# Moving a matmul's streamed operand by 192 bytes: x and its forms from 224 to 32 modulo 256 in a two-layer hybrid decoder

## The chip, the cores and the metric

The kernel runs on one core of one Trainium2 chip. The metric is the device time of one execution in microseconds (us); shown is the median of three runs. The engines are TensorE (PE; its weight loads are a row of their own, PEld), VectorE (DVE), ScalarE (ACT), GpSimd (POOL) and SyncE (SP), which issues the loads from device memory.

## What is computed

Two decoder layers over 512 tokens of width 1024, in float32. Each layer is a half-step SwiGLU FFN, a token mixer (sparse attention, NSA, in layer 0; the gated recurrence HGRN2 in layer 1) and a second half-step FFN, each followed by a layer norm:

```python
def _swiglu(x, w_gate, w_up, w_down):
    return (jax.nn.silu(x @ w_gate) * (x @ w_up)) @ w_down

for i in range(DEPTH):
    x = _layer_norm(alpha * x + 0.5 * _swiglu(x, ffn1 of layer i), ...)
    y = _nsa(x, ...) if kind == 0 else _hgrn2(x, ...)
    x = _layer_norm(alpha * x + y, ...)
    x = _layer_norm(alpha * x + 0.5 * _swiglu(x, ffn2 of layer i), ...)
```

The FFN's inner width is 2816. The mixers project x by `w_in` (NSA: queries, keys, values, gates; HGRN2: four times 1024 columns) and their output by `w_out`.

## The kernel before, in words

Every float32 operand of a large product is held as two parts, `hi` and `lo` (ACT rounds a copy, DVE subtracts), and `mm3` (lines 126 to 130) makes a product of three matmuls: hi by hi, lo by hi or hi by lo, and so on. A row such as `ps<-xh,whi` names the moving operand first (streamed column by column) and then the stationary one (loaded ahead as weights). A matmul has 128 rows of contraction and 256 or 512 columns.

x is kept transposed in `xh` and `xl` (made by `new_xt`, line 79), in a pool `xt` at the upper end of SBUF. Weights come through SP into `raw`, and are split into the ring `whi`/`wlo` or, in the FFN, into two further buffers `xhi`/`xlo`; the last weights of a `down` or of an output projection go into a pool `wl`.

The FFN (`ffn_body`, line 248) takes 22 blocks of 128 inner columns in two halves, 12 and then 10. Blocks go in pairs. The first pair of the first half is `plain_pair`. All others are `seven`: seven products of half-size blocks instead of eight, on x's four quarters (moving `xh`/`xl`) and on three sums of quarters, the forms `t0h` to `t2l` (variable `tf`, in a pool `mid`). A product is 2 x 4 calls of `mm3` on 256 columns. The weights' sums are formed in `fr`, also in `mid`, as are `sg`, `p1`, `q2`, `q3` and `c`. So the first half has one plain pair and five of `seven`, the second half five of `seven`; after each half, `down` multiplies the 12 or 10 blocks of `h` (stationary parts `xhi`/`xlo`) by `w_down` (moving, 512 columns), 8 PSUM banks at once.

Elsewhere x is moving in `proj_t` (512 columns in two pieces; NSA's compression, keys and queries, HGRN's queries) and stationary in `tok_proj` (HGRN's other three projections, weights moving, 512 columns), in NSA's value projections (256 and 304 columns) and in NSA's output projection, for which `o_t` writes the attention's output into `xh`/`xl`. HGRN's output projection has its own stationary tiles, `oth`/`otl`.

PE's program stands in the order in which it is written; the other engines' order is set by a scheduler.

`gap` (line 74) takes a tile that nobody uses, so that what stands behind it in its pool starts later.

Of the kernel before, what the change touches and what calls it, by code (L numbers as in the profile page):

```python
# [55 lines left out]
class Trunk:  # L56
# [22 lines left out]
    def new_xt(self):  # L79

        self.free_xt()
        self.xt = ExitStack()
        pool = self.xt.enter_context(self.tc.tile_pool(name="xt", bufs=1, side="right", reuse_waits="tile"))
        self.xh = pool.tile([P, 2, NK, 2 * P], F32R, name="xh")
        self.xl = pool.tile([P, 2, NK, 2 * P], F32R, name="xl")

    def xr(self, k, c0=0, c1=NT):

        s = slice(c0 // 2, c1 // 2)
        return self.xh[:, s, k, :], self.xl[:, s, k, :]  # L90
# [158 lines left out]
    def ffn_body(self, pool, wg, wu, wd, gb_idx, out):  # L249
        nc = self.nc  # L250
        self.gap(pool, 128)
        h = pool.tile([P, 12, T], F32, name="h")

        self.wx = pool, 2
        w3 = [w.rearrange("(k p) f -> p k f", p=P) for w in (wg, wu)]
        LASTU = 4
        with ExitStack() as es:
            mid = es.enter_context(self.tc.tile_pool(name="mid", bufs=1, reuse_waits="tile"))
            self.gap(mid, 192)
            tf = [[mid.tile([P, 4, 256], F32R, name=f"t{n}{x}") for x in "hl"] for n in range(3)]  # L260

            hq = h.rearrange("p j t -> p (j t)")
            xb = hq[:, 2048:4096].rearrange("p (a k t) -> p a k t", a=2, k=4)
            f1, f2 = (hq[:, 1024 * n : 1024 * n + 1024].rearrange("p (k t) -> p k t", k=4) for n in (4, 5))
            for half, (f0, nf) in enumerate(((0, 12), (12, 10))):
                for pr in range(nf // 2):
                    g = f0 // 2 + pr
                    if g < NSTD:
                        if g == 0:
                            for k in range(2):  # L270
                                ks = slice(4 * k, 4 * k + 4)
                                nc.gpsimd.tensor_tensor(xb[:, k], self.xh[:, 0, ks].bitcast(F32), self.xl[:, 0, ks].bitcast(F32), op=ALU.add)
                            self.forms = xb, f1, f2
                        self.plain_pair(mid, w3, g, h[:, 2 * pr : 2 * pr + 2, :])
                        if g == 0:
                            self.forms = None
                            for (hi, lo), src in zip(tf, (f1, f2, xb[:, 0])):
                                self.split(hi, lo, src)
                        if g == NSTD - 1:
                            self.split(self.xh[:, 1, 0:4], self.xl[:, 1, 0:4], xb[:, 1])  # L280
                    else:
                        self.seven(mid, tf, w3, g, h[:, 2 * pr : 2 * pr + 2, :], g >= NSTD + 2)
                if half == 0:
                    banks = self.down(wd, h, f0, nf, nf, None)
                    for c in range(NT):
                        for x in range(2):
                            s = slice(512 * x, 512 * x + 512)
                            nc.vector.scalar_tensor_tensor(self.x[c][:, s], self.x[c][:, s], 2.0 * ALPHA, banks[c][x], op0=ALU.mult, op1=ALU.add)
        with ExitStack() as es:
            wl = es.enter_context(self.tc.tile_pool(name="wl", bufs=4, reuse_waits="tile"))  # L290
            gb = self.ln_params(*gb_idx, [wl.tile([P, D], F32, name=n, bufs=1) for n in ("lng", "lnb")])
            banks, last = self.down(wd, h, f0, nf, nf - LASTU, wl)
            self.finish(last, banks, gb, 4.0 * LN_EPS, out)
# [971 lines left out]
```

## Time and profile before

| | |
|---|---|
| median of 3 runs | 2103.89 us (2103.47 to 2104.97) |
| the profiled execution | 2099.54 us, its span 2097.8 us |
| PE busy | 2055.2 us, 98% |
| PEld busy | 1885.4 us, 90% |
| DVE busy | 1418.3 us, 68% |
| ACT busy | 976.1 us, 47% |
| granted clock of TensorE, mean | 0.995 |

Busy is the time in which an engine has at least one instruction in hand. Matmuls overlap: the record of one lasts longer than the distance to the next. The idle time in a row of the groups is that of the engine ahead of these instructions, with what ended it.

The first FFN's halves of `seven` lie at about 30 to 133 and 199 to 297 us, the second FFN's at 725 to 833 and 897 to 996, the third's at 1070 to 1176 and 1242 to 1341, the fourth's at 1765 to 1868 and 1934 to 2034; a `down` follows each. NSA runs from 353 to 705 and HGRN from 1396 to 1745.

### The profile page before, as it was taken

Reading aid. Unit: us, or ns where it says so; the run is one execution under the profiler, and the core shown is the slowest. Engines: PE = TensorE matmul, PEld = TensorE weight load, DVE = VectorE, ACT = ScalarE, POOL = GpSimd, SP = SyncE. Lnnn points to the kernel's source line nnn. Section 1 sums busy time; section 2 is a strip of 40 time slices with the busy share of each in tenths; the row PEclk is TensorE's granted clock in tenths of the full one; section 3 lists DMA queues with packets and bytes.
Section 4 is the critical chain, followed back from the end, with each engine's and each line's share of the span. In section 5 each row is a group of like instructions: output and inputs, shape, how many; then the busy total and the mean of one; then the engine's idle time right before and its main releaser. Section 6 shows DMA issues by size and latency. Waiting matters only on the chain.

```text
span 2097.8 us, 34590 instructions
## 1 busy us (share of the span) xinstructions
PE 2055.2 (98%) x14277; PEld 1885.4 (90%) x14277; DVE 1418.3 (68%) x2124; ACT 976.1 (47%) x1570; POOL 217.2 (10%) x321
## 2 busy tenths in 40 slices
PE   8999999999999999999999999999999999999998
PEld 8998998879898899899899989988788989998996
DVE  8946855377775896486598467664636858955864
ACT  5543552255565354255345335435536734543551
POOL 1000002001122300000110000021321213000002
PEclk9999999999999999999999999999999999999999
DMA  5441342231011145133234412512231023342331
GB/s 181 122 150 51 102 145 76 82 110 41 31 31 51 61 125 157 48 113 115 67 121 124 138 57 86 172 60 90 82 116 31 2 71 101 115 147 61 101 121 41
DMA packets 138762, 194.00 MB, mean 92 GB/s; under 512 B 8571, under 2 KB 117435, under 8 KB 138604
## 3 DMA queue, kind: packets, MB, share of 16 engines
q1 hardware_dynamic: 138604, 191.79, 29.6%
q8 instruction: 112, 1.84, 0.4%
q14 instruction: 46, 0.38, 0.1%
HBM read 189.58 MB, written 2.19 MB: 91 GB/s over the span
## 4 chain that ended last, share of the span: by engine, by line
PE 83%; DVE 10%; POOL 2%; ACT 2%; issue 1%; DMA 1%; DVEq 0%; POOLq 0%; SPq 0%; ACTq 0%
PE ps L128 23%; PE ps L130 23%; PE ps L129 23%; PE po L820 3%; DVE wlo L113 2%; PE ps L804 2%; PE ps L1148 1%; DVE raw L350 1%; PE sc L771 1%; PE sc L772 1%; DVE st L201 1%; DVE x L200 1%; PE ps L543 1%; DVE xl L113 1%; ACT whi L112 1%
## 5 line engine op out<-in xcount | busy, mean ns | idle before, releaser
L113 DVE TENSOR_TENSOR wlo<-raw,whi 128x1024 fp32r<-128x1024 f32 (+1 forms) x253 | 315.2, 1250 | 275.0 <-ACT whi L112 274.3
L112 ACT ACTIVATE whi<-raw 128x1024 fp32r<-128x1024 f32 (+1 forms) x253 | 265.6, 1055 | 359.7 <-PE ps L130 164.5
L128 PE MATMUL ps<-xh,whi 128*128 128x256 f32 (+1 forms) x1120 | 332.9, 297 | 3.0 <-ACT whi L112 1.6
L130 PE MATMUL ps<-xh,wlo 128*128 128x256 f32 (+1 forms) x1120 | 331.1, 296 | 2.3 <-DVE wlo L113 2.3
L129 PE MATMUL ps<-xl,whi 128*128 128x256 f32 (+1 forms) x1120 | 331.0, 296 | 1.2 <-DVE xl L113 1.2
L130 PE MATMUL ps<-whi,xlo 128*128 128x512 f32 x704 | 274.4, 390 | 1.5 <-DVE xlo L113 1.5
L128 PE MATMUL ps<-whi,xhi 128*128 128x512 f32 x704 | 274.4, 390 | 0.0
L129 PE MATMUL ps<-wlo,xhi 128*128 128x512 f32 x704 | 274.0, 389 | 0.0
L130 PEld LDWEIGHTS ps<-xh,wlo 128*128 128x128 f32 x1120 | 212.3, 190 | 10.2 <-DVE wlo L113 2.8
L128 PEld LDWEIGHTS ps<-xh,whi 128*128 128x128 f32 x1120 | 210.8, 188 | 11.8 <-ACT whi L112 2.0
L129 PEld LDWEIGHTS ps<-xl,whi 128*128 128x128 f32 x1120 | 211.0, 188 | 8.9 <-DVE xl L113 1.8
L128 PE MATMUL ps<-xh,xhi 128*128 128x256 f32 x640 | 180.2, 282 | 7.3 <-DVE q L404 7.2
L112 ACT ACTIVATE whi<-fr 128x1024 fp32r<-128x1024 f32 x120 | 126.7, 1059 | 118.6 <-PE ps L129 83.8
L129 PE MATMUL ps<-xl,xhi 128*128 128x256 f32 x640 | 179.8, 281 | 0.0
L130 PE MATMUL ps<-xh,xlo 128*128 128x256 f32 x640 | 179.8, 281 | 0.0
L113 DVE TENSOR_TENSOR wlo<-fr,whi 128x1024 fp32r<-128x1024 f32 x120 | 146.8, 1224 | 47.4 <-ACT whi L112 47.1
L130 PEld LDWEIGHTS ps<-whi,xlo 128*128 128x128 f32 x704 | 132.2, 188 | 30.7 <-DVE xlo L113 3.2
L129 PEld LDWEIGHTS ps<-wlo,xhi 128*128 128x128 f32 x704 | 132.2, 188 | 26.8
L128 PEld LDWEIGHTS ps<-whi,xhi 128*128 128x128 f32 x704 | 132.2, 188 | 26.8
L350 DVE TENSOR_TENSOR raw<-fr 128x1024 f32<-128x1024 f32 x120 | 145.8, 1220 | 13.1 <-DMA fr<-in_ffn_w_up_dram 11.4
L113 DVE TENSOR_TENSOR xlo<-h,xhi 128x1024 fp32r<-128x1024 f32 x44 | 53.9, 1226 | 111.8 <-ACT xhi L112 111.8
L128 PEld LDWEIGHTS ps<-xh,xhi 128*128 128x128 f32 x640 | 121.6, 190 | 8.1 <-DVE q L404 7.8
(267 smaller groups left out, 4737.7 us busy)
## 6 DMA issues: line engine op xcount, KB each, us to landing
raw<-in_ffn_w_down_dram SPq DMA_DIRECT2D x88, 512.0 KB, 3.5
fr<-in_ffn_w_gate_dram SPq DMA_DIRECT2D x80, 512.0 KB, 4.0
fr<-in_ffn_w_up_dram SPq DMA_DIRECT2D x80, 512.0 KB, 5.0
raw<-in_hgrn_w_in_dram SPq DMA_DIRECT2D x32, 512.0 KB, 4.2
raw<-in_nsa_w_in_dram SPq DMA_DIRECT2D x18, 512.0 KB, 3.9
raw<-in_ffn_w_gate_dram SPq DMA_DIRECT2D x8, 512.0 KB, 5.4
raw<-in_ffn_w_up_dram SPq DMA_DIRECT2D x8, 512.0 KB, 4.5
raw<-in_nsa_w_out_dram SPq DMA_DIRECT2D x8, 512.0 KB, 3.4
```

Source lines behind the costliest of these rows:

```text
L112: a = self.nc.scalar.activation(hi, src, AF.Copy)
L113: b = self.nc.vector.tensor_tensor(lo, src, hi.bitcast(F32), op=ALU.subtract)
L128: mm(out, l[0], r[0], start=start, stop=False)
L129: mm(out, l[0], r[1], start=False, stop=False)
L130: mm(out, l[1], r[0], start=False, stop=stop)
L200: nc.vector.scalar_tensor_tensor(x[:, s], x[:, s], float(scale), banks[h], op0=ALU.mult, op1=ALU.add)
L201: nc.vector.bn_stats(st[:, h, :], x[:, s])
L350: tt(out, x, y, op=op)
L543: nc.tensor.matmul(ph, w1[:, j, :], self.ap(z[:, 0:1], 2 * j, [[16, 129]]), start=j == 0, stop=j == 15)
L771: nc.tensor.matmul(sc[:, t - ts[0], :], l, kh[t][g][:, :n], start=True, stop=False)
L804: nc.tensor.transpose(p[:, j * P : j * P + P], pf[:, (b0 + j) * P : (b0 + j + 1) * P], self.ident)
L820: nc.tensor.matmul(po[:, ii, t, :], pt[:, t * (i + 1) + j, :], v[j][:, t, g, :], start=j == 0, stop=j == i)
```

## The change

One gap leaves pool `mid`, and one of the same size enters pool `xt`:

```diff
@@ new_xt
         self.xh = pool.tile([P, 2, NK, 2 * P], F32R, name="xh")
         self.xl = pool.tile([P, 2, NK, 2 * P], F32R, name="xl")
+        self.gap(pool, 192)
@@ ffn_body
             mid = es.enter_context(self.tc.tile_pool(name="mid", bufs=1, reuse_waits="tile"))
-            self.gap(mid, 192)
             tf = [[mid.tile([P, 4, 256], F32R, name=f"t{n}{x}") for x in "hl"] for n in range(3)]
```

Pool `xt` ends at the upper end of SBUF, so the new gap moves `xh` and `xl` down by 192 bytes (196576 to 196384 and 212960 to 212768); what stands in `mid` moves down by 192 as well. No other tile moves. The starts of the tiles modulo 256 bytes in the two programs (the steps within these tiles are multiples of 256):

| tiles | before | after |
|---|---|---|
| `xh`, `xl` | 224 | 32 |
| `t0h` to `t2l`, `fr`, `sg`, `p1`, `q2`, `q3`, `c` (pool `mid`) | 224 | 32 |
| `raw`, the ring `whi`/`wlo`, the FFN's `xhi`/`xlo`, `h`, its `wl`, x itself | 32 | 32 |
| `wl` of NSA's output projection | 0 | 0 |
| `wl` of HGRN's output projection, `oth`/`otl` | 160 | 160 |

The instructions and their order are the same on every engine. Two waits differ, both in the last FFN, since tiles of `mid` now lie over other tiles of the stage before: ACT's split into `t1h` loses a wait for a load, and on SP's queue the third pair of loads of `fr` gains one for PE. SP's rows there, before:

```order
L343 DMA fr<-in_ffn_w_gate_dram 128x4x256 [waits PE_49]
L343 DMA fr<-in_ffn_w_up_dram 128x4x256 [waits DMAHW6_49]
L343 DMA fr<-in_ffn_w_gate_dram 128x4x256 [waits DMAHW7_49]
L343 DMA fr<-in_ffn_w_up_dram 128x4x256
L343 DMA fr<-in_ffn_w_gate_dram 128x4x256
L343 DMA fr<-in_ffn_w_up_dram 128x4x256 [waits DMAHW2_49]
```

and after (names ending in `_49` are the program's semaphores: PE's, and those of single load queues):

```order
L343 DMA fr<-in_ffn_w_gate_dram 128x4x256 [waits PE_49]
L343 DMA fr<-in_ffn_w_up_dram 128x4x256 [waits DMAHW6_49]
L343 DMA fr<-in_ffn_w_gate_dram 128x4x256 [waits DMAHW7_49]
L343 DMA fr<-in_ffn_w_up_dram 128x4x256
L343 DMA fr<-in_ffn_w_gate_dram 128x4x256 [waits PE_49]
L343 DMA fr<-in_ffn_w_up_dram 128x4x256 [waits DMAHW2_49]
```

Nothing moved; the fifth load waits for PE, for the last but one matmul of HGRN's output projection, for which the first of these loads already waited in the program before.

## Rows read from the trace of the kernel before

**Rows 1.** The page, busy time of PE, its share and instructions.

```profile
PE 2055.2 (98%) x14277; PEld 1885.4 (90%) x14277; DVE 1418.3 (68%) x2124; ACT 976.1 (47%) x1570; POOL 217.2 (10%) x321
```

**Rows 2.** The page, the chain that ended last, by engine.

```profile
PE 83%; DVE 10%; POOL 2%; ACT 2%; issue 1%; DMA 1%; DVEq 0%; POOLq 0%; SPq 0%; ACTq 0%
```

**Rows 3.** Windows of `seven`: length, busy (count) of PE, PEld, DVE, ACT, POOL, clock, DMA.

```profile
200.00:296.00 96.00, 96.00 (x817) 96.00 (x817) 71.98 (x74) 51.39 (x69) 0.00 (x0) 1.00 0.33 99
...
900.00:990.00 90.00, 90.00 (x766) 90.00 (x766) 66.94 (x69) 48.08 (x66) 0.00 (x0) 1.00 0.32 95
...
1100.00:1170.00 70.00, 70.00 (x620) 70.00 (x619) 55.20 (x60) 38.17 (x51) 0.00 (x0) 1.00 0.48 148
1245.00:1340.00 95.00, 95.00 (x809) 95.00 (x809) 70.71 (x73) 51.18 (x68) 0.00 (x0) 1.00 0.32 97
...
1936.00:2030.00 94.00, 94.00 (x801) 94.00 (x800) 70.60 (x74) 50.61 (x68) 0.00 (x0) 1.00 0.32 96
```

**Rows 4.** First of PE's groups, 1100 to 1170 us: count, busy, mean ns, idle before.

```profile
L128 PE MATMUL ps<-xh,whi 128*128 128x256 f32 x64 | 17.7, 276 | 0.0
```

**Rows 5.** The same group of PE, 200 to 296 us.

```profile
L128 PE MATMUL ps<-xh,whi 128*128 128x256 f32 x78 | 21.9, 281 | 0.0
```

**Rows 6.** Timeline of PE at the seam of `down` and `seven`: start, duration.

```profile
198.89 0.39 PE L130 MATMUL ps<-whi,xlo 128*128 128x512 f32 x1
199.12 0.28 PE L128 MATMUL ps<-xh,whi 128*128 128x256 f32 x1
199.24 0.28 PE L129 MATMUL ps<-xl,whi 128*128 128x256 f32 x1
199.35 0.28 PE L130 MATMUL ps<-xh,wlo 128*128 128x256 f32 x1
```

**Rows 7.** Windows, PE alone: `down`, `tok_proj`, HGRN's `proj_t` (PE, clock, DMA).

```profile
1557.50:1587.50 30.00, 30.00 (x130) 1.00 0.28 88
...
1415.00:1497.00 82.00, 82.00 (x360) 1.00 0.30 93
136.00:196.00 60.00, 60.00 (x267) 1.00 0.17 52
```

**Rows 8.** Timeline of PE, HGRN's output projection, ring weights: first and last of 14.

```profile
1708.14 0.39 PE L128 MATMUL ps<-whi,oth 128*128 128x512 f32 x1
...
1711.17 0.40 PE L129 MATMUL ps<-wlo,oth 128*128 128x512 f32 x1
```

**Rows 9.** The same, weights from `wl`: first and last of 9.

```profile
1724.15 0.39 PE L129 MATMUL ps<-wlo,oth 128*128 128x512 f32 x1
...
1725.96 0.39 PE L128 MATMUL ps<-whi,oth 128*128 128x512 f32 x1
```

**Rows 10.** Groups of PE by form, whole span; one of the three lines of `mm3`.

```profile
L128 PE MATMUL ps<-whi,xh 128*128 128x512 f32 x256 | 100.7, 393 | 0.0
...
L128 PE MATMUL ps<-xh,whi 128*128 128x512 f32 x160 | 64.1, 400 | 0.3 <-DVE qs L713 0.3
```

**Rows 11.** Groups of PE, 748.1 to 750.3 us, behind a stall.

```profile
L128 PE MATMUL ps<-xh,xhi 128*128 128x256 f32 x7 | 2.1, 296 | 2.5 <-DVE q L404 2.5
L129 PE MATMUL ps<-xl,xhi 128*128 128x256 f32 x7 | 2.0, 281 | 0.0
```

**Rows 12.** Groups of PE, 752 to 755 us.

```profile
L129 PE MATMUL ps<-xl,xhi 128*128 128x256 f32 x6 | 1.7, 276 | 0.0
```

**Rows 13.** The page, DVE's subtraction by its source.

```profile
L113 DVE TENSOR_TENSOR wlo<-raw,whi 128x1024 fp32r<-128x1024 f32 (+1 forms) x253 | 315.2, 1250 | 275.0 <-ACT whi L112 274.3
...
L113 DVE TENSOR_TENSOR wlo<-fr,whi 128x1024 fp32r<-128x1024 f32 x120 | 146.8, 1224 | 47.4 <-ACT whi L112 47.1
```

**Rows 14.** Timelines of PE and SP at the fourth FFN's start.

```profile
1744.99 0.39 PE L129 MATMUL ps<-wlo,oth 128*128 128x512 f32 x1
...
1747.47 0.77 SPq L343 DMA_DIRECT2D fr<-in_ffn_w_gate_dram  x1
```

## The prediction

> **What bounds the kernel now.** I read the page first: PE is busy 98% of the 2097.8 us span [rows 1] and has 83% of the chain that ended last [rows 2]. Busy is no measure of pace, since a matmul's record includes its way through the array, so I asked at which distance matmuls start. In a stretch where PE has no idle time, the pace is (length of the window + length of one record) / count, because a record that reaches over the window's edge is counted too.
>
> The main loop of each FFN is `seven`, with 256 columns per matmul, run five times before the first `down` and five times after it: same code, same shapes, same buffers. Before `down`, in the row of 1100 to 1170 us: (70.00 + 0.276) / 620 = 113.35 ns [rows 3, 4]. After it: (96.00 + 0.281) / 817 = 117.85 ns, and by the same sum 117.86, 117.78 and 117.70 ns in the other three FFNs [rows 3, 5]. Nobody is waited for in either: idle before each group is 0.0 [rows 4, 5], the granted clock is 1.00, PE is busy for the whole window [rows 3]. So the slow halves do not wait for an instruction; each matmul itself takes 4.4 ns more. The seam shows when it begins: `down` ends at 0.23 us a matmul of 512 columns, and from the very next one, without a gap, starts are 0.11 to 0.12 us apart [rows 6], the pace of the whole half.
>
> What the slow stretches share is the offset, modulo 256 bytes, of their two operands, which PE streams (moving) and loads (stationary) at the same time: PEld is as busy as PE in rows 3. The table of offsets stands in the section on the change. In pace per 512 columns:
> - `down`, 32 against 32: (60.00 + 0.389) / 267 = 226.2 ns [rows 7]
> - `tok_proj`, moving 32, stationary 224: (82.00 + 0.391) / 360 = 228.9 ns [rows 7]
> - `proj_t`, moving 224, stationary 32: (30.00 + 0.394) / 130 = 233.8 ns [rows 7]
> - the HGRN output projection, stationary 160: with the weights of the ring, at 32, 13 intervals take 3.03 us, 233 ns [rows 8]; with the weights of `wl`, at 160, 8 intervals take 1.81 us, 226 ns [rows 9].
>
> The last pair is the best experiment in this trace: same line, shape and stationary tiles, and only the moving operand's offset differs. Equal offsets run at 226 ns, unequal ones at 229 to 234.
>
> **The change part by part.** It moves `xh`/`xl` and all of pool `mid` from 224 to 32, so that every pair of `seven`, `proj_t` and `tok_proj` becomes 32 against 32. No instruction is added, removed or reordered.
>
> (a) Second halves of the FFNs: 5 pairs x 7 products x 8 x 3 = 840 matmuls, four times, 3360. If they run at the first halves' pace, each gives 117.8 - 113.4 = 4.4 ns: 14.8 us. All of it lies on the path, as PE never idles there. Cover: DVE, the next busiest, has 71.98 of 96 us; at the first halves' pace it has 55.20 of 70, 79%, and PE still has no idle time there [rows 3], so the inputs arrive in time. The bounds are 0 (the pace stays) and 14.8; I take 14.8, since equal offsets in rows 7 and 9 are the nearest rows.
>
> (b) `tok_proj`: 3 x 192 = 576 of the 768 matmuls of 512 columns whose stationary is x [rows 10] (256 on each of three lines; the other 192 are NSA's output projection), each 228.9 - 226.2 = 2.7 at most and 228.9 - 226.7 = 2.2 by two intervals of the 113.35 pace: 1.3 us.
>
> (c) `proj_t` on 512 columns: 160 x 3 = 480 matmuls [rows 10]. 144 are HGRN's queries, on the path: 7 ns each, 1.0 us. 48 stand in NSA's compression: 0.3 us. 288 stand among the attention's units, where PE also waits for others; between 0 and 2.0 us, I take 1.0.
>
> (d) NSA's value projections, 96 of 256 and 96 of 304 columns with x stationary: no clean stretch; between 0 and the 4.4 ns of the second halves, 0.8 us, which I take. Output projection, 192: the half whose weights come from the ring becomes 32 against 32, 96 x 5 ns = 0.5 us; the other half has `wl` at 0 against 224 now and against 32 then, a pair that no row shows: between -0.6 and +0.6 us, 0 taken.
>
> (e) First halves are at 113.35 already: 0.
>
> (f) `fr`, the `sg` tiles and `c` move too, and DVE and ACT read or write them. The same subtraction takes 1250 ns from `raw` (at 32) and 1224 ns from `fr` (at 224) [rows 13]; DVE has slack, and I put it at nothing.
>
> (g) On SP's queue the third pair of loads of the last FFN gains a wait for PE. It waits for the last but one matmul of the HGRN output projection; the first pair, ahead of it in the queue, waited for that already. It was issued at 1747.47 us, 2.48 us after that matmul started [rows 14]. Behind it stand the other loads of that FFN. Price 0.
>
> Sum: 14.8 + 1.3 + 2.3 + 1.3 = 19.7 us. The profiled execution took 2099.54 us (span 2097.8 and 1.7 around it); the median of the three timed runs is 2103.89, 4.4 more, and I take the gain from the median: 2084.2.
>
> **The rivals.**
>
> *The pace depends on how a stretch is entered, not on the offsets.* For it: the first halves have the same unequal offsets and run at 113 ns. The middle of FFN 2's first half shows the jump: after a stall of 2.5 us the records are 281 ns long, the slow kind, and three microseconds later, after another short stall, 276 again [rows 11, 12]. Then second halves, entered from `down` without a stall, keep 117.8 and only (b) to (d) gain, 4.9 us: 2099. Against it: `down` never runs slow, whether entered from a fast or a slow stretch; two paces are seen only where offsets differ.
>
> *Equal offsets are good at 512 columns and bad at 256 (slower).* At 256 columns the weight load has no spare time: PEld is busy for all of each window in rows 3, with a load for each matmul. If a load that begins on the same offset as the stream loses the turn there, all of `seven` goes to the slow pace: the first halves too, about 1000 matmuls x 4 x 4.4 ns = 17.6 us lost, second halves unchanged, 4.9 gained elsewhere: 2116.6. No row has 256 columns at equal offsets in a steady stretch, so this is open. It decides once more than some 1100 of the 4000 matmuls (4.9 us / 4.4 ns) turn slow while the second halves stay. Against it: `down` enters each load in the same way, its first 256 columns run beside a whole load, and they lose nothing.
>
> *The offsets do nothing.* The paces would come from something else that differs between these stretches (the kind of access, or the tiles' places modulo more than 256): 2104. Rows 8 and 9 speak against it, two stretches 13 us apart with the same stationary.
> The Trainium skill speaks for this rival. Its page TensorE: Matmul & The Clock Gate, section Step-by-step: what each phase is for, says that TensorE reads SBUF through two independent ports and that loading the next weights takes no read bandwidth from the running matmul; SBUF — State Buffer, section Who interferes with whom, says that PE never waits on anyone. By these rules the offsets of the two operands cost nothing and the time stays 2104; the trace disagrees, with 233 against 226 ns in rows 8 and 9.
>
> **How the numbers follow.** Forecast 0.73, history 0.10, slower 0.10, nothing 0.07. Own range of the forecast: all bounds at their best (288 attention matmuls and the open pair in full) give 21.3 us, 2082.5; all at their worst beside (a) give 16, 2088; with a microsecond for the measurement 2081 to 2089. To hold 8 in 10, the range reaches up to the history case: 2081 to 2099.5. A measurement of this kernel can tell about 0.2%, 4.2 us, from no change. Faster by more: the forecast and, since 4.9 is just over, six tenths of the history case, 0.79. Same: the rest of that and the nothing case, 0.11. Slower: 0.10.
>
> **What would show it.** In the changed kernel's trace, windows in the second halves (about 200 to 292 us) should count 847 matmuls in 96 us instead of 817, with records of 276 ns instead of 281; `tok_proj` should count 363 in 82 us instead of 360 and HGRN's `proj_t` 134 in 30 instead of 130; the first halves should stay at 620 in 70. The HGRN output projection and `down`, whose operands don't move, should keep their pace. If the second halves keep 281 ns, (a) is wrong and the history rival right; if the first halves show 281, the slower rival is. If PE shows idle time before groups of the second halves, the gain has met DVE or the loads.

## The result, and the profile after

The changed kernel takes 2126.38 us (median of 5 runs, 2121.21 to 2127.32) where the kernel before takes 2104.49 (5 runs beside it, 2103.47 to 2106.57): a ratio of 1.0098, 95% interval 1.0083 to 1.0113. It is 1% slower; forecast was 1% faster. In the profiled executions the span goes from 2097.8 to 2119.4 us, 21.6 more, and the mean granted clock is 0.997 (0.995 before).

The answers to [rows 1, 2], in the page of after: the same instructions, and PE busy for 28.8 us more. It still has the chain that ended last.

```profile
PE 2084.0 (98%) x14277; PEld 1918.3 (91%) x14277; DVE 1420.5 (67%) x2124; ACT 976.6 (46%) x1570; POOL 216.6 (10%) x321
...
PE 84%; DVE 9%; ACT 2%; POOL 2%; issue 1%; DMA 0%; DVEq 0%; POOLq 0%; ACTq 0%
```

The windows of `seven` in after answer [rows 3] (same columns: length, then busy and count of PE, PEld, DVE, ACT, POOL, then clock and DMA). The first two lie in first halves, the others in second halves.

```profile
20.00:50.00 30.00, 30.00 (x253) 30.00 (x252) 29.92 (x33) 17.09 (x19) 0.00 (x0) 1.00 0.33 102
...
1130.00:1180.00 50.00, 50.00 (x419) 50.00 (x418) 36.34 (x39) 26.45 (x36) 0.00 (x0) 1.00 0.46 144
...
208.00:304.00 96.00, 96.00 (x802) 96.00 (x801) 70.06 (x72) 50.54 (x68) 0.00 (x0) 1.00 0.31 95
912.00:1002.00 90.00, 90.00 (x752) 90.00 (x752) 65.62 (x68) 47.43 (x64) 0.00 (x0) 1.00 0.31 95
```

The groups of PE in 208 to 304 us are the answer to [rows 4, 5] (count, busy, mean ns, idle before; `mm3` is one line further down in after):

```profile
L129 PE MATMUL ps<-xh,whi 128*128 128x256 f32 x72 | 20.4, 283 | 0.0
...
L129 PE MATMUL ps<-t2h,whi 128*128 128x256 f32 x40 | 11.3, 283 | 0.0
```

By the sum of the prediction, (length + one record) / count, a second half now runs at (96.00 + 0.283) / 802 = 120.05 ns a matmul, where it had 117.85; a first half at (50.00 + 0.283) / 419 = 120.01, where it had 113.35. Read matmul by matmul, the distance from one start to the next is 120 ns for 638 of the 672 matmuls on x and for all 360 on the forms in the first FFN's first half. So there is one pace for all of `seven`, and it is slower than both paces of before. Nobody waits in the second halves (idle 0.0, PE busy 96.00 of 96.00, clock 1.00).

The seam of `down` and `seven`, the answer to [rows 6]:

```profile
204.56 0.39 PE L130 MATMUL ps<-wlo,xhi 128*128 128x512 f32 x1
204.78 0.39 PE L131 MATMUL ps<-whi,xlo 128*128 128x512 f32 x1
205.01 0.28 PE L129 MATMUL ps<-xh,whi 128*128 128x256 f32 x1
205.12 0.28 PE L130 MATMUL ps<-xl,whi 128*128 128x256 f32 x1
205.24 0.28 PE L131 MATMUL ps<-xh,wlo 128*128 128x256 f32 x1
205.36 0.28 PE L129 MATMUL ps<-xh,whi 128*128 128x256 f32 x1
```

And the windows of `down`, `tok_proj` and HGRN's `proj_t`, PE alone, the answer to [rows 7]:

```profile
146.00:203.00 57.00, 57.00 (x254) 1.00 0.18 56
1430.00:1510.00 80.00, 80.00 (x355) 1.00 0.30 91
1576.00:1604.00 28.00, 28.00 (x125) 1.00 0.30 94
```

These are (57.00 + 0.389) / 254 = 225.9, (80.00 + 0.389) / 355 = 226.4 and (28.00 + 0.389) / 125 = 227.1 ns; from start to start they are 226 or 227 in most cases and 226.7 to 227.0 on average in all three. At 512 columns equal offsets did what was forecast: 228.9 and 233.3 became 226.7 to 227.0.

Where the 21.6 us are, by the starts of the first matmul of each stage in the two traces (us; a stage with what follows it up to the next):

| stage | before | after | difference |
|---|---|---|---|
| first half, FFN 1 / 2 / 3 / 4 | 123.94 / 123.60 / 124.96 / 124.41 | 129.87 / 127.50 / 128.43 / 127.86 | +5.93 / +3.90 / +3.47 / +3.45 |
| second half, each of four | 98.93 | 100.79 | +1.86 |
| `down`, first of each FFN | 65.30 | 65.31 | 0 |
| second `down`, norm and NSA | 409.10 | 407.83 | -1.27 |
| second `down`, norm and HGRN | 404.41 | 403.10 | -1.31 |

First halves +16.75, second halves +7.44, mixers -2.58: 21.6.

The first halves would have lost more. Some 4000 matmuls got 6.6 ns longer, some 26 us by the distances in the traces, but some 9 us of it was covered: PE waited there for DVE and ACT, and with a slower PE these waits shrink. The waits of PE in the second FFN's first half of after (us in total, times, longest) show one where [rows 11] have 2.5 us on the same line:

```profile
PE ps L129 <- DVE q L404: 1.1, 1, 1.1
```

### The profile page after: what moved, and what is told of

It reads as the page before. It is cut to its first block, busy times and chain, and to the rows that moved or that the text cites. A ratio compares the mean times of both kernels' runs of the same rounds, so it can differ in the third digit from the quotient of the medians.

```text
span 2119.4 us, 34590 instructions
## 1 busy us (share of the span) xinstructions
PE 2084.0 (98%) x14277; PEld 1918.3 (91%) x14277; DVE 1420.5 (67%) x2124; ACT 976.6 (46%) x1570; POOL 216.6 (10%) x321
## 4 chain that ended last, share of the span: by engine, by line
PE 84%; DVE 9%; ACT 2%; POOL 2%; issue 1%; DMA 0%; DVEq 0%; POOLq 0%; ACTq 0%
PE ps L129 24%; PE ps L131 24%; PE ps L130 24%; PE po L820 3%; DVE wlo L114 2%; PE ps L804 2%; PE ps L1148 1%; PE sc L772 1%; PE sc L771 1%; DVE st L202 1%; DVE x L201 1%; DVE raw L350 1%; DVE xl L114 1%; PE ps L543 1%; DVE x L217 1%
## 5 line engine op out<-in xcount | busy, mean ns | idle before, releaser
L114 DVE TENSOR_TENSOR wlo<-fr,whi 128x1024 fp32r<-128x1024 f32 x120 | 146.8, 1224 | 53.9 <-ACT whi L113 53.0
L205 POOL TENSOR_SCALAR lm<-mv 128x1 f32<-128x1 f32 x24 | 18.4, 768 | 1065.7 <-DVE mv L203 1065.6
```

The lines of the kernel that those rows point to most:

```text
L114: b = self.nc.vector.tensor_tensor(lo, src, hi.bitcast(F32), op=ALU.subtract)
```

## The experiments

All change the kernel before. "Difference" is the start of the moving operand minus that of the stationary one, modulo 256 bytes: 192 in `seven` of the kernel before (224 against 32), 0 in that of after.

**Half of the change: x at 32, the forms stay at 224.**

```diff
-        self.xl = pool.tile([P, 2, NK, 2 * P], F32R, name="xl")
+        self.xl = pool.tile([P, 2, NK, 2 * P], F32R, name="xl"); self.gap(pool, 192)
```

> Half of the change: xh and xl start at 32 modulo 256, the forms and the rest of pool mid stay at 224. Theory P, the pace of a matmul follows from the offsets of its own two operands: the four products of seven on x's quarters take 120.0 ns a matmul as in the changed kernel, the three on the forms 113 to 118 as before; the 512-column products on x take 226.7. Against the changed kernel 3/7 of 7360 matmuls are 2 to 7 ns shorter, so 2108 to 2119 us. Rival Q, one pace for a whole stretch (a lock that any disturbance sets): all products of a stretch share one pace between 113 and 120, with no step between a product on x and one on a form.

Measured: 2105.54 us, ratio 1.0003 (0.9993 to 1.0012), below the expected range. Groups of PE in a second half, 202 to 296 us:

```profile
L130 PE MATMUL ps<-xh,wlo 128*128 128x256 f32 x80 | 22.6, 283 | 0.0
L128 PE MATMUL ps<-xh,whi 128*128 128x256 f32 x80 | 22.6, 282 | 0.0
...
L129 PE MATMUL ps<-t2l,whi 128*128 128x256 f32 x40 | 11.1, 277 | 0.0
...
L130 PE MATMUL ps<-t2h,wlo 128*128 128x256 f32 x40 | 11.1, 276 | 0.0
```

Within one call of `seven` the records change from product to product: 283 ns (starts 120.0 ns apart) on x, 276 or 277 (113.3, after three matmuls of 116 to 121) on the forms. So the pace goes with the pair of operands, as one of the theories said. What none of them had: the forms, whose offsets did not move, run at 113.3 in the second halves too, where they ran at 117.8 before. That gain pays for the loss on x, and the total stands still.

**The other half: the forms at 32, x stays at 224.**

```diff
-            self.gap(mid, 192)
+            pass
```

> The other half of the change: pool mid at 32, xh and xl stay at 224. Theory P: the three products on the forms take 120.0 ns a matmul, the four on x's quarters 113 to 118; tok_proj stays at 228.9 and proj_t at 233.3. Before plus 4000 x 3/7 x 6.6 ns (11 us) plus 3360 x 3/7 x 2.2 ns (3 us), less what slower matmuls hide of DVE's waits: 2109 to 2119 us. Rival Q: one common pace in a stretch.

Measured: 2102.13 us, ratio 0.9991 (0.9979 to 1.0003), below the expected range. Groups of PE in the same stretch:

```profile
L128 PE MATMUL ps<-xh,whi 128*128 128x256 f32 x77 | 21.3, 277 | 0.0
L129 PE MATMUL ps<-xl,whi 128*128 128x256 f32 x77 | 21.3, 277 | 0.0
...
L128 PE MATMUL ps<-t1h,whi 128*128 128x256 f32 x40 | 11.3, 283 | 0.0
L129 PE MATMUL ps<-t1l,whi 128*128 128x256 f32 x40 | 11.3, 283 | 0.0
```

The mirror image: now the forms are at 120 and x's products, at the unchanged difference 192, fall from 117.8 to 113.3, all but the first product of each half, which has `down` ahead of it and stays at 117.8. Either half alone costs nothing, both together 1%. That can't be a sum of costs per operand; at difference 192 there must be two paces, and products at 120 ahead of them lead to the better one.

**Other differences.** Both gaps were resized together, so that x and its forms start at another multiple of 32. For 64, for example:

```diff
-        self.xl = pool.tile([P, 2, NK, 2 * P], F32R, name="xl")
+        self.xl = pool.tile([P, 2, NK, 2 * P], F32R, name="xl"); self.gap(pool, 160)
-            self.gap(mid, 192)
+            self.gap(mid, 32)
```

> x and its forms at 160, a distance of 128 from the weights at 32. Theory A, at 256 columns the matmul loses most where the two operands start on the same offset and least where they are farthest apart, at 512 columns the other way round: seven at 113.4 ns in first and second halves, proj_t and tok_proj at 233 to 234; some 2093 us. Rival B, distance 128 is bad at any width, as in HGRN's output projection with 234 ns: seven at 118 to 120 or more, 2112 to 2135 us.

> x and its forms at 96, moving minus stationary 64 in seven. NSA's value projections of the kernel before have the same difference (weights at 32 moving, x at 224) and run at 117.7 ns throughout. Theory A (a function of the difference, moving minus stationary, modulo 256): 117.7 in both halves, some 2110 us. Rival C (only the size of the distance counts, 64 as before's 192): two paces again, 113.3 in first and 117.8 in second halves, some 2104 us.

> x and forms at 192, difference (moving minus stationary) 160, between 128 (119) and 192 (113.3 or 117.8). Theory S, only the 64-byte step in which each operand starts counts, and 192 starts the same step as 224: paces as in the kernel before, 113.3 and 117.8, about 2104 us. Theory F, every 32 bytes count: a pace of its own between 113.3 and 120, 2089 to 2130 us.

> x and forms at 0, difference 224, between 192 (113.3 or 117.8) and 0 (120). Theory S (64-byte steps: 0 starts the same step as the weights' 32): 120 ns as in the changed kernel and 226.7 for 512 columns, about 2126 us. Theory F (every 32 bytes count): a pace of its own between 113.3 and 120.

> x and forms at 64, difference 32. Theory S (64-byte steps; 64 starts the same step as 96): 117.8 ns throughout as in both_96, about 2114 us. Theory F: a pace of its own between 117.8 and 120, or lower.

> x and its forms at 128, weights at 32: difference 96, the last of the eight steps of 32. The other seven gave 120.0 (0), 116.7 (32), 117.8 (64), 118.7 (128), 118.7 (160), 113.3 or 117.8 (192), 118.3 ns (224) in second halves. A step between its neighbours gives 117.8 to 118.7 in both halves and 2112 to 2124 us; a second good place like 192 would show 113.3 in first halves at least and 2085 to 2105 us.

One profiled execution each; beside them the kernel before had medians of 2104.04 to 2107.88 us and single executions from 2099.51 to 2113.94, so the paces tell more than the times. Mean distance from start to start at 256 columns, without stalls:

| x and forms at | difference | first halves, ns | second halves, ns | time, us |
|---|---|---|---|---|
| 32 (after) | 0 | 119.9 to 120.0 | 120.0 | 2121.21 |
| 64 | 32 | 116.7 to 117.6 | 116.7 | 2106.34 |
| 96 | 64 | 117.8 | 117.8 | 2114.26 |
| 128 | 96 | 120.0 | 120.0 | 2129.56 |
| 160 | 128 | 118.7 to 118.9 | 120.0 | 2127.43 |
| 192 | 160 | 117.3 to 117.7 | 118.7 | 2115.74 |
| 224 (before) | 192 | 113.3 to 113.5 | 117.8 | 2099.54 |
| 0 | 224 | 118.3 | 118.3 | 2116.27 |

The best and the worst of the new ones in a window of a second half, PE alone, at 64:

```profile
208.00:298.00 90.00, 90.00 (x773) 1.00 0.32 100
```

and at 128:

```profile
208.00:298.00 90.00, 90.00 (x752) 1.00 0.29 89
```

(90.00 + 0.28) / 773 is 116.8 and (90.00 + 0.28) / 752 is 120.1 ns. One expectation held: with x at 96 the pace is 117.8, that of NSA's value projections at the same difference. Three fell. That only equality is bad fell with the first of these runs (difference 128 is as bad in second halves); that the pace has coarser steps than 32 bytes fell with x at 192, 0 and 64; and the last, x at 128, expected between its neighbours at 117.8 to 118.7, came out at 120.0, in the slowest of these executions (2129.56 us). I have no formula for the column of paces. Nor is 192 the only difference with two paces: at 128 and 160, too, second halves keep a slower one than first halves, and at 32 the third FFN's first half goes from 116.7 to 117.8 at 1101 us, behind a short stall, and stays there. In these runs the roles don't matter, only the difference: NSA's value projections, in which x is stationary and the weights move, run at 117.75 ns in the kernel before (their difference is 64) and at 113.85 with x at 96, where it becomes 192.

**What sets the pace at difference 192.** Six extra matmuls of 256 columns stand ahead of the first product of each second half (`kick` is set for its first pair); both operands are weights at 32, and the result is overwritten by the product that follows:

```diff
+        if kick:
+            for _ in range(6):
+                nc.tensor.matmul(a[:, :256], w[1][0][:, 0, 0, :], w[1][0].rearrange("p m k f -> p (m k f)")[:, :256], start=True, stop=True, skip_group_check=True)
         product(1, a, True)
```

> The kernel before, all offsets as they are, with six extra matmuls of 256 columns ahead of the first product of each second half (moving and stationary both the weights at 32, result overwritten): 24 in all, some 2.8 us. Theory H, at a difference of 192 two paces can last and the stretch ahead sets which: behind matmuls of 256 columns on equal offsets the products on x were fast in every half of x224_forms32. So the second halves run at 113.3 ns instead of 117.8, 3360 x 4.4 ns = 14.9 us less 2.8: about 2092 us. Rival, the second halves are slow for another reason than how they are entered (what DVE, ACT or the loads do there): 117.8 stays and the time is some 2107 us.

Measured: 2095.04 us where the kernel before had 2107.88 beside it, ratio 0.9931 (0.9914 to 0.9949): faster, with 24 instructions more. The seam, timeline of PE:

```profile
201.63 0.39 PE L130 MATMUL ps<-whi,xlo 128*128 128x512 f32 x1
201.86 0.88 PE L395 MATMUL ps<-whi 128*128 128x256 f32 x6
202.57 0.29 PE L128 MATMUL ps<-xh,whi 128*128 128x256 f32 x1
202.69 0.28 PE L129 MATMUL ps<-xl,whi 128*128 128x256 f32 x1
202.81 0.28 PE L130 MATMUL ps<-xh,wlo 128*128 128x256 f32 x1
202.93 0.28 PE L128 MATMUL ps<-xh,whi 128*128 128x256 f32 x1
```

From start to start: 113 ns for the first extra one, 120 for the other five, then 121, 122, 116, 114 and from there 113.3 to the end of the half. Windows of this kernel, the first in the second half, the others early and late in the first FFN's first half:

```profile
204.00:294.00 90.00, 90.00 (x796) 1.00 0.31 97
20.00:50.00 30.00, 30.00 (x268) 1.00 0.33 101
60.00:130.00 70.00, 70.00 (x597) 1.00 0.47 148
```

The second half has (90.00 + 0.276) / 796 = 113.4 ns instead of 117.8; all four do, at unchanged offsets. And a first half can lose the fast pace on its way: 113.0 ns before, (70.00 + 0.281) / 597 = 117.7 after one matmul, at 54.70 us, that starts 60 ns late, in a stretch where the profile names nobody that PE waited for. It did not come back until the half's end. The third FFN's first half lost it at 1125 us, there behind a wait of 0.5 us for ACT. So both paces last, and what comes before decides.

A control, against the one just shown: the same six with x at 224 as the moving operand, so at difference 192 themselves:

```diff
-                nc.tensor.matmul(a[:, :256], w[1][0][:, 0, 0, :], w[1][0].rearrange("p m k f -> p (m k f)")[:, :256], start=True, stop=True, skip_group_check=True)
+                nc.tensor.matmul(a[:, :256], w[1][0][:, 0, 0, :], x[1][0][:, 0, :], start=True, stop=True, skip_group_check=True)
```

> Control for the run with six extra matmuls. Same six extra matmuls of 256 columns at the same four places (ahead of the first product of each second half, result overwritten), same stationary operand, but the moving one is x at 224 instead of a weight at 32: difference 192 as everywhere in `seven`. Theory H (at difference 192 two paces last, and a stretch at equal offsets is what throws PE from the slow into the fast one): nothing flips, the extra ones run at 117.8 ns themselves, the second halves stay at 117.8 ns, and the time is the before's plus 4 x 6 x 0.118 = 2.8 us, so ratio 1.001 (0.999 to 1.003). Rival M (any extra matmuls on one and the same stationary operand, or the overwritten bank, would do): second halves at 113.3 ns, ratio 0.993 as with the equal offsets.

Measured: 2108.21 us, ratio 1.0016 (1.0002 to 1.0030). The window in the second half:

```profile
204.00:294.00 90.00, 90.00 (x766) 1.00 0.31 94
```

(90.00 + 0.281) / 766 = 117.9 ns: nothing flips. It is the equal offsets of the extra matmuls, not that they are there. Extra matmuls at a third difference were not tried.

One extra matmul at equal offsets ahead of every `seven`, again against the run with six:

```diff
-            for _ in range(6):
+            for _ in range(1):
...
-                        self.seven(mid, tf, w3, g, h[:, 2 * pr : 2 * pr + 2, :], g >= NSTD + 2, half == 1 and pr == 0)
+                        self.seven(mid, tf, w3, g, h[:, 2 * pr : 2 * pr + 2, :], g >= NSTD + 2, True)
```

> One extra matmul of 256 columns at equal offsets (weights by weights, both at 32, result overwritten) ahead of each of the 40 calls of `seven`, else the kernel before. If one is enough to set the fast pace: second halves at 113.3 ns from their first pair on (14.9 us less), slips in the course of a half end with the pair in which they come, cost 40 x (0.12 + 0.02) = 5.6 us; 2094 to 2098 where the before has 2104 to 2108, ratio 0.995. If one is not enough: paces as in before (117.8 in second halves) and the cost is added, ratio 1.002 to 1.003.

Measured: 2111.61 us, ratio 1.0031 (1.0020 to 1.0042), the cost and no gain:

```profile
204.00:294.00 90.00, 90.00 (x767) 1.00 0.31 94
```

One is not enough; six are. Where between them the limit lies was not tried.

**Using it.** If 24 matmuls at equal offsets lead into the fast pace, one product of each `seven` can do it without extra instructions. Only `t2`, the moving operand of the second product, goes to 32:

```diff
-            self.gap(mid, 192)
-            tf = [[mid.tile([P, 4, 256], F32R, name=f"t{n}{x}") for x in "hl"] for n in range(3)]
+            pass
+            t2 = [mid.tile([P, 4, 256], F32R, name=f"t2{x}") for x in "hl"]; self.gap(mid, 192); tf = [[mid.tile([P, 4, 256], F32R, name=f"t{n}{x}") for x in "hl"] for n in range(2)] + [t2]
```

> Of the three forms only t2 (both parts, moving operand of the second product of each `seven`) goes to 32; x, t0, t1 and the rest of the pool stay at 224. By theory H each `seven` sets its own pace: t2's 24 matmuls at 120.0 ns, the other six products at 113.3 in all eight halves, but the first product of each second half at 117.8. Cost against all at 113.3: 40 x (24 x 6.67 ns + 20 ns) = 7.2 us; against the profiled before: second halves 14.9 - 3.6 - 0.4 = 10.9 us gained, first halves 3.6 us lost, 7.3 us less in all, so 2092 beside a profiled 2099.5, ratio 0.995 to 0.998. Rival: the pace is set once at the start of a half, by the seam behind `down`, and products on x and t0, t1 stay at 117.8 in second halves: ratio 1.003 (7 us of t2's at 120 in first halves and 2 ns more in second halves).

Measured: 2091.80 us (2090.97 to 2092.97, 5 runs) where the kernel before had 2104.68 beside it (2099.51 to 2111.94, 23 runs), ratio 0.9936 (0.9920 to 0.9951): faster than the kernel before by 0.6%, and than the changed one (2126.38, from the first comparison) by 1.6%. Groups of PE in a second half, 204 to 294 us:

```profile
L128 PE MATMUL ps<-xh,whi 128*128 128x256 f32 x72 | 19.9, 276 | 0.0
...
L128 PE MATMUL ps<-t2h,whi 128*128 128x256 f32 x40 | 11.3, 282 | 0.0
...
L128 PE MATMUL ps<-t1h,whi 128*128 128x256 f32 x40 | 11.1, 277 | 0.0
```

t2's product has records of 282 ns (starts 120 apart), x's and t1's of 276 and 277 (113.3 apart); the first product of a second half still runs at 117.8. Second halves take 96.12 us instead of 98.93, first halves 0.1 to 1.8 us more than before, 8.6 us less in all in the profiled executions (7.3 expected, from 2099.5 to 2092; it was 2090.97). The medians differ by 12.9, and the runs lie within 2.0 us of each other where those of the kernel before spread over 12.4. My reading is that in most executions of the kernel before some first halves slip, and that here a slip ends with the next `t2`. The control's trace shows such slips in first halves that are those of the kernel before: three of its four run at 116.4 to 116.6 ns on average, the other at 113.35. The one trace of the kernel before is of an execution of 2099.54 us, among its shortest, so that its longer ones slip in the same way is argued, not shown.

## Why the prediction was wrong, point by point

**(a) and (e), `seven`: wrong, and this is the step that failed.** The prediction took equal offsets at 512 columns [rows 7, 9] as the nearest rows for 256 columns, and wrote 113.4 for the second halves and no change for the first. Both became 120.0. So (a), whose bounds of 0 and 14.8 us left no side on which second halves lose, cost 7.44 us instead of gaining 14.8, and (e), put at 0 because the first halves were "at 113.35 already", cost 16.75. The number of columns is what differs: the six extra matmuls are weights by weights, both at 32, the offsets of `down`, and at 256 columns they run 120 ns apart while `down` at 512 stands at 226.7, twice 113.3.

Why the same offsets are good at one size and bad at the other is argued, not shown. The rows of PEld in after show one difference, `seven` in 208 to 304 us:

```profile
L129 PEld LDWEIGHTS ps<-xh,xhi 128*128 128x128 f32 x76 | 14.6, 192 | 0.0
```

and `down` in 150 to 200 us:

```profile
L130 PEld LDWEIGHTS ps<-wlo,xhi 128*128 128x128 f32 x74 | 13.9, 188 | 2.9
```

At 512 columns PEld has 2.9 us of idle time before 74 loads, 39 ns each; at 256 columns there is none. So a load that gets longer beside a running stream would cost time at 256 columns and none at 512. The prediction's second rival had this argument ("At 256 columns the weight load has no spare time"), and I gave it 0.10, on the ground that `down`'s first 256 columns run beside a whole load and lose nothing. They may lose; there it can't be seen. But the argument isn't the whole: HGRN's `proj_t` of the kernel before, in 1557.5 to 1587.5 us at difference 192, has loads with 2.0 us of idle time before 43, 47 ns each, and its matmuls still stand 233.3 ns apart.

```profile
L130 PEld LDWEIGHTS ps<-xh,wlo 128*128 128x128 f32 x43 | 8.0, 187 | 2.0
```

So offsets also cost something where loads have slack. The starts don't tell which of the two is held up: the next load starts 2 to 5 ns after each matmul at either size and at every pace read here, so the distance from a load to its own matmul grows with the pace whatever the cause. What in the array or its memory makes the difference was not settled.

**The first halves' fast pace was not evidence for equal offsets.** They run at difference 192 like the second halves; the prediction explained the second halves' 117.8 ns by offsets and left the first halves' 113.35, at the same offsets, without an explanation. Both paces belong to difference 192, and the runs with six extra matmuls show that what precedes decides. The trace of the kernel before shows it too: first halves begin at the slow pace as well. In the second FFN the first matmuls stand 117.8 ns apart; then eight transposes of x (matmuls on the identity, `ident`) interrupt the plain pair, and behind them, from 711.2 us on, it is 113.3:

```profile
709.75 0.28 PE L129 MATMUL ps<-xl,whi 128*128 128x256 f32 x1
709.86 0.28 PE L130 MATMUL ps<-xh,wlo 128*128 128x256 f32 x1
709.98 1.03 PE L159 MATMUL ps<-ident,x 128*128 128x128 f32 x8
710.77 0.37 PE L128 MATMUL ps<-xh,whi 128*128 128x256 f32 x1
...
711.21 0.28 PE L128 MATMUL ps<-xh,whi 128*128 128x256 f32 x1
711.32 0.28 PE L129 MATMUL ps<-xl,whi 128*128 128x256 f32 x1
```

The fourth FFN turns at its first transposes too (1749 us), the first and the third only at later ones (at 21.5 and 1061.3 us). A second half has no transposes and no wait, and keeps 117.8. Why one interruption turns the pace and another doesn't is open. The history rival was right on this point, wrong in that it took the pace to be independent of offsets: in after no other pace than 120.0 lasts at difference 0, whatever precedes. Its observation on [rows 11, 12] was the clue.

**The slower rival** had the sign and the place, `seven` at 256 columns; its mechanism is open, as said. Its price, 2116.6, is 9.8 below what was measured. It took the slow pace to be 117.8 (it is 120.0, so second halves lose too, 7.4 us), counted the first halves' loss at 17.6 (some 26 by distances, 16.75 after what the waits covered) and the mixers' gain at 4.9 (2.6). That 17.6 comes so near 16.75 is luck: the step was 6.6 ns and not 4.4, and the cover was left out.

**(b) and (c)**: right in mechanism and size per matmul, 226.7 to 227.0 in both. By distances `tok_proj` gave 1.2 us (1.3 forecast), HGRN's queries 0.9 (1.0), NSA's `proj_t` 1.8. **(d)**: wrong; NSA's value projections went from 117.75 to 119.7 (difference 64 to 0), for the reason of (a), and cost 0.2 us instead of gaining 0.8; its output projection stayed the same within 0.1 us. Of all that, the two mixers' stages show 2.6 us; that the rest met other waits is likely and not shown.

**(f)** right: the subtraction from `fr`, now at 32, takes the 1224 ns that it took at 224 [rows 13], so the 26 ns between it and the one from `raw` never were the offset's.

```profile
L114 DVE TENSOR_TENSOR wlo<-fr,whi 128x1024 fp32r<-128x1024 f32 x120 | 146.8, 1224 | 53.9 <-ACT whi L113 53.0
```

**(g)** right: in after the load with the new wait is issued 1.57 us after the fourth FFN's first matmul (1763.31 and 1761.74 us), 0.55 behind the load ahead of it, as in before.

**That the offsets do nothing** is refuted by every run here. The Trainium skill, on whose page TensorE: Matmul & The Clock Gate (section Step-by-step: what each phase is for) the rival leaned, says that loading the next weights steals no read bandwidth from the running matmul. The traces disagree: with a load beside each matmul, where the two operands start moves the pace from 113.3 to 120.0 ns at 256 columns and from 226.7 to 234.3 at 512, at a granted clock of 1.00.

**Two sums of the prediction** don't come out of its own numbers, and neither matters to the result: at 113.35 ns a second half's 96 us would have counted 849 matmuls and not 847, and the parts at their worst beside (a) add up to 17.3 us and not 16.

## What to carry to other kernels

Where a matmul is so short that weight loads follow each other without a gap, its pace depended here on the start of the moving operand against the stationary one modulo 256 bytes, and rows with longer matmuls, whose loads have slack, gave another order of offsets: measure at the size that is used. Before blaming a property for a slow stretch, ask whether the fast stretch has the same property; if it does, what came ahead of the stretch or interrupted it is a suspect, and a short disturbance put ahead of it is a cheap test. A move of all operands to "the good place" can lose what a move of a single one wins: here one form of three at equal offsets (2091.80 us) beats none (2104.68) and all (2126.38).

## What the runs showed of the chip that I had not expected

- In multiples of 32 bytes no difference was faster from entry to end than 116.7 ns; only 192 reaches 113.3, and it has a second pace, 117.8, that lasts for a whole half of an FFN (98.93 us). A delay of 60 ns took a half from the fast to the slow one. Six matmuls at equal offsets, the slowest pairs of all, turned the slow into the fast one, and one did not; so did eight transposes in the kernel before, though not each time.
- Differences of 0 and 96 both give 120.0 on average, but not alike: at 0 each distance is 120 ns, at 96 they go round through 125, 116, 123, 119, 120 and 117.
- At 512 columns the order is another one: 226.7 to 227.0 ns at difference 0, 228.9 to 229.1 at 64, 232.4 at 128 (233.3 in HGRN's output projection), 234.2 to 234.3 at 160, and 233.3 at 32, 96, 224 and 192, the last of which at 256 columns is the only one that reaches 113.3.
